# Block products for six inner tiles of the first feed-forward block, its state-space preparation in the last 44 products, and a re-ordered mixer

## The chip, the core and the metric

The kernel runs on one core of a Trainium2 chip. The metric is the device time of one execution in microseconds (us); three runs of the kernel before took 1043.52, 1045.11 and 1045.87 us, median 1045.11. The engines are called as in the profile: PE (TensorE matmul), PEld (its weight loads), DVE (VectorE), ACT (ScalarE), POOL (GpSimd), SP (the queue that issues the loads).

## What is computed

One block on x (512 frames x 1024 channels, float32) with a conditioning vector c: three sub-layers, each a normalised and modulated h with a gated residual.

```
mod = silu(c) @ w_ada + b_ada                       # 9 vectors of 1024
h = modulate(rms_norm(x, g1), mod[0], mod[1]);  x += 0.5*mod[2]*swiglu(h, w1_in, w1_out)
h = modulate(rms_norm(x, g2), mod[3], mod[4])
u_pool, u_ssm, gl_pool, gl_ssm = split(h @ w_in)
y = sigmoid(gl_pool)*(multiscale_pool(u_pool) @ w_pool_up) + sigmoid(gl_ssm)*(s5_mixer(u_ssm) @ w_ssm_up)
x += mod[5] * (y @ w_out)
h = modulate(rms_norm(x, g3), mod[6], mod[7]);  x += 0.5*mod[8]*swiglu(h, w3_in, w3_out)
return rms_norm(x, g_final)
```

swiglu(h) = (silu(a) * b) @ w_out with a, b = h @ w_in, 2816 inner channels: 22 *inner tiles* of 128, each with an a and a b product. The S5 part is a complex diagonal state space, 32 groups of 64 states; its discretised coefficients and their powers up to 127 frames are computed from the parameters in the kernel ("state-space preparation").

## The kernel before

**Layout.** Activations lie transposed: channels on the 128 partitions, 512 frames along the free axis, so h is 8 tiles of 128x512. Weights come from memory in float32, each tile is split into a high part (ACT cast, `wh`, L1327, in `split_hi`) and a low part (DVE subtraction, `wl`, L1335, in `split_lo`), and so are the activations (HH/HL for h, GHA/GLA and GC for the gated inner tiles). `mm3` (L265 to L268) makes each product from three matmuls: high x high, high x low, low x high.

**Units.** All work is a list of `Unit`s, each with its weights, its matmuls and what follows. The main loop (L1371 on) emits, for unit i: `pre`, the split of the weights of unit i+2 and loads beyond it (`prefetch`), the matmuls, `post`, perhaps a step of the adaLN dots (`ada_step`: one load of 512 KB and one 128x1024 dot on DVE, L132, with a small update of gates or scales), and in the first block one entry of the list `fill`. Every engine works through its instructions in the order in which they are emitted. A *plain* unit has 1024 weight columns, 24 matmuls of 512 columns; an *out* unit of n inner tiles has 3n.

**First block** (`ffn(0, ...)`, units 0 to 76). `group6` (L281) takes seven column tiles at once while h is still being made (`make_h1`, L222); then come plain units in `BLOCKS` of 6, 5, 5 and 6 inner tiles, each followed by out units that add to the residual X (L660); the last two, in `tail` (L340), are split into halves of 256 columns, interleaved with the next norm (column sums L202, row broadcast L216). `keep_warm(WARM[i])` (L1365 to L1368) puts dummy matmuls between the steps of the first norm.

**State-space preparation.** `fill` starts behind unit 18: the parameter loads (`ssm_load`), then 181 small DVE operations, 10 a unit (`SMALL`, recorded in `small`, all shown at L721) from unit 20 on. POOL builds tables of powers by doubling (`ssm_table(k)`, L912 to L917, k = 0 to 6, each six operations, the largest 128x1024), which use scratch that also holds results of the small operations. Then four batches: `ssm_batch_pool(b)` (L930 to L944) on POOL, and four units later `ssm_batch_pe(b)` on PE (transposes L951, products L956) with `ssm_batch_m(b)` (copies and diagonals, L969 to L971). A batch has six units: POOL's part is in the first and PE's in the last of them.

**Mixer** (`mixer()`, order written by hand at L1217 on). u units make the pool input, pf units the state-space input, gp and gs the gates; `si` (`ssm_in`, L1015), `sc` (`ssm_scan`, L1031: scans L1037) and `so` are the state-space steps on PE, DVE and POOL; `pw` multiplies the pooled tiles by pool_w (`pw_unit`, L1160 and the splits that follow), and `up` multiplies the result by w_pool_up.

**Third sub-layer** (`ffn_seven`, L458). Here 18 inner tiles are made in nine pairs by seven block products instead of eight (Winograd's form, 2x2 blocks): h is also needed as sums and differences of its blocks (`h_sums`, POOL, L248 to L251; split later), and weight blocks likewise (POOL, L517 to L519). `product` (L495 to L499) makes three 256-column matmuls; a pair has 56 products, in four halves of two units each (`half_units`: `split1`, `split2`), with sums behind them in `post1`, `done_a` and `done_b`. The second operands of a half lie in four slots.

Of the kernel before, what the change touches and what calls it, by code (L numbers as in the profile page):

```python
# [16 lines left out]
P = 128  # L17
# [3 lines left out]
BLOCKS = ((0, 6), (6, 11), (11, 16), (16, 22))  # L21
# [5 lines left out]
SMALL = 10  # L27
WARM = (6, 7, 1, 3)
# [17 lines left out]
class Unit:  # L46
    def __init__(self, src, cols, mm, pre=None, post=None):
# [3 lines left out]
        self.kind = 0  # L51
# [3 lines left out]
def block_kernel(ctx, tc, a, out):  # L55
# [96 lines left out]
    ada_jobs = []  # L152
# [10 lines left out]
    ada_loaded, ada_done = [0], [0]  # L163

    def ada_step():
# [6 lines left out]
        while ada_loaded[0] < len(ada_jobs) and ada_loaded[0] - ada_done[0] < 2:  # L172
            ada_load(ada_jobs[ada_loaded[0]][0])
            ada_loaded[0] += 1
# [47 lines left out]
    def make_h1(s, k, part):  # L222
# [6 lines left out]
        S.activation(out=HH[:, k, cs], in_=t[:, cs], func=AF.Identity, bias=shift_col(s, k))  # L229
        if s == 2:  # L230
# [10 lines left out]
    def h_sums(kp):  # L241
        if not sums:
            sums["h"] = big("SH", [P, 4, 4, T // 2], F32R, "PM")
            sums["l"] = big("SL", [P, 4, 4, T // 2], F32R, "QM")
        t = TB.rearrange("p r q c -> p (r q c)")[:, 1024 * kp:1024 * kp + 1024].rearrange("p (s t) -> p s t", s=4)
        f0, f1 = HF[2 * kp % 4], HF[(2 * kp + 1) % 4]
# [5 lines left out]
        late_splits.append(lambda: put_split(sums["h"][:, kp], sums["l"][:, kp], t))  # L252

    def make_h2(s, k, t, part):
# [5 lines left out]
        if s == 2 and k % 2 and made[k] == T and made[k - 1] == T and k // 2 not in made.setdefault("sums", []):  # L260
            made["sums"].append(k // 2)
            h_sums(k // 2)
# [195 lines left out]
    def ffn_seven(s, w6, win, wout, wend):  # L458
# [1054 lines left out]
```

## Time and profile before

| | |
|---|---|
| median of three runs | 1045.11 us (1043.52 to 1045.87) |
| profiled execution | 1044.0 us, of which the span 1042.2 |
| PE, DVE, ACT, POOL busy | 1026.7, 727.5, 392.0, 348.7 us |
| matmul groups with 512 and 256 columns, L266 to L268 | largest two: 536 and 308 per line |
| seven-product matmuls, L499 | three operand forms of 216 are the largest |
| weight splits wl, L1335 | 164, 195.3 us |
| adaLN dots, L132 | 50, 72.9 us |

In a row of the profile, `out<-in` are the tiles written and read (buffer numbers left out), then shape, count, and, in brackets, how long the engine had been idle and what released it. Spans of a window are followed by busy times of the five engines, the granted PE clock (1.00 is full), the share of the DMA engines and GB/s.

### The profile page before, as it was taken

The numbers are of one execution on the slowest core, as the hardware profiler recorded it, in microseconds if no ns is written. First come the engines' busy times: TensorE is split into PE (matmuls) and PEld (weight loads), VectorE is DVE, ScalarE is ACT, GpSimd is POOL, SyncE is SP. The second block draws the span as 40 slices with busy tenths as digits, with TensorE's granted clock in tenths as the row PEclk, the third lists the DMA queues.
The fourth block names the chain that finished last, engine by engine and source line by source line (L and its number), as shares of the span: only waits on it lengthen the run. The fifth ranks groups of instructions, "written<-read, shape, count | busy, mean of one in ns | idle before, by whom it ended". The sixth has DMA issues, their size and how long they took to land.

```text
span 1042.2 us, 14304 instructions
## 1 busy us (share of the span) xinstructions
PE 1026.7 (99%) x5514; PEld 872.5 (84%) x5514; DVE 727.5 (70%) x1127; ACT 392.0 (38%) x595; POOL 348.7 (33%) x309
## 2 busy tenths in 40 slices
PE   9999999999999999998999999999999999999996
PEld 7788888788888889886888887887899989988986
DVE  6956678989665655669924588365899948975843
ACT  4252222222232243584143333255545424432443
POOL 0000200499652411045600000133587705832312
PEclk9999999999999999999999999999999999999999
DMA  9664544445426432412336455222332522431222
GB/s 348 222 207 157 185 162 136 147 143 187 149 101 218 152 107 66 131 52 81 101 102 205 147 193 182 61 74 79 128 125 86 189 61 76 151 109 45 83 76 81
DMA packets 46310, 138.23 MB, mean 133 GB/s; under 512 B 5281, under 2 KB 9505, under 8 KB 46242
## 3 DMA queue, kind: packets, MB, share of 16 engines
q1 hardware_dynamic: 46242, 137.32, 38.9%
q8 instruction: 43, 0.70, 0.3%
q14 instruction: 25, 0.20, 0.1%
HBM read 134.15 MB, written 3.15 MB: 132 GB/s over the span
## 4 chain that ended last, share of the span: by engine, by line
PE 89%; DVE 5%; ACT 3%; issue 1%; DMA 0%; SPq 0%; DVEq 0%; ACTq 0%
PE ps L266 21%; PE ps L268 21%; PE ps L267 20%; PE ps L499 17%; PE ps L295 7%; DVE wl L1335 1%; ACT U L1010 1%; DVE ev L719 1%; ACT wh L1327 1%; PE ps L956 1%; DVE ev L225 1%; PE ps L1055 1%; ACT HH L229 1%; PE ps L202 1%; DVE PM L1037 1%
## 5 line engine op out<-in xcount | busy, mean ns | idle before, releaser
L1335 DVE TENSOR_TENSOR wl<-raw,wh 128x1024 fp32r<-128x1024 f32 (+4 forms) x164 | 195.3, 1194 | 83.9 <-ACT wh L1327 83.3
L1327 ACT CAST wh<-raw 128x1024 fp32r<-128x1024 f32 (+4 forms) x166 | 150.8, 913 | 162.2 <-PE ps L267 111.3
L268 PE MATMUL ps<-HH,wl 128*128 128x512 f32 (+1 forms) x536 | 208.1, 388 | 2.3 <-DVE wl L1335 2.3
L266 PE MATMUL ps<-HH,wh 128*128 128x512 f32 (+1 forms) x536 | 208.9, 390 | 0.0
L267 PE MATMUL ps<-HL,wh 128*128 128x512 f32 (+1 forms) x536 | 208.2, 388 | 0.0
L268 PEld LDWEIGHTS ps<-HH,wl 128*128 128x128 f32 x536 | 100.5, 187 | 25.8 <-DVE wl L1335 2.8
L267 PEld LDWEIGHTS ps<-HL,wh 128*128 128x128 f32 x536 | 100.5, 188 | 23.3 <-DVE HL L719 0.7
L266 PEld LDWEIGHTS ps<-HH,wh 128*128 128x128 f32 x536 | 100.5, 188 | 23.1 <-issue 0.4
L268 PE MATMUL ps<-GHA,wl 128*128 128x512 f32 (+1 forms) x308 | 118.3, 384 | 1.3 <-DVE wl L1335 1.3
L266 PE MATMUL ps<-GHA,wh 128*128 128x512 f32 (+1 forms) x308 | 118.7, 385 | 0.0
L267 PE MATMUL ps<-GLA,wh 128*128 128x512 f32 (+1 forms) x308 | 117.9, 383 | 0.0
L660 DVE SCALAR_TENSOR_TENSOR X<-ps,MOD,X 128x512 f32<-128x512 f32 (+1 forms) x78 | 55.1, 706 | 64.8 <-PE ps L268 64.7
L186 POOL TENSOR_TENSOR ACC<-ACC,ev 128x512 f32<-128x512 f32 x15 | 19.7, 1311 | 222.3 <-ACT ev L185 222.3
L132 DVE CUSTOM_DVE_ANT_0 ADA<-ADA,C,COL 128x1024 f32<-128x1024 f32 x50 | 72.9, 1458 | 0.0
L268 PEld LDWEIGHTS ps<-GHA,wl 128*128 128x128 f32 x308 | 57.8, 188 | 14.9 <-DVE wl L1335 2.4
L267 PEld LDWEIGHTS ps<-GLA,wh 128*128 128x128 f32 x308 | 57.8, 188 | 12.7 <-DVE GLA L272 0.3
L266 PEld LDWEIGHTS ps<-GHA,wh 128*128 128x128 f32 x308 | 57.8, 188 | 12.5 <-issue 0.4
L499 PE MATMUL ps<-SH,wl 128*128 128x256 f32 x216 | 60.5, 280 | 0.0
L499 PE MATMUL ps<-SH,wh 128*128 128x256 f32 x216 | 60.3, 279 | 0.0
L499 PE MATMUL ps<-SL,wh 128*128 128x256 f32 x216 | 60.2, 279 | 0.0
L517 POOL TENSOR_TENSOR MISC<-MISC 128x512 f32<-128x512 f32 x18 | 31.7, 1760 | 80.2 <-DMA MISC<-w_f_in 80.2
L271 ACT CAST GHA<-ev 128x512 fp32r<-128x512 f32 x24 | 14.9, 621 | 80.0 <-DVE ev L412 72.7
(253 smaller groups left out, 2136.4 us busy)
## 6 DMA issues: line engine op xcount, KB each, us to landing
ADA<-w_ada SPq DMA_DIRECT2D x50, 512.0 KB, 3.5
raw<-w_f_in SPq DMA_DIRECT2D x39, 512.0 KB, 4.3
raw<-w_f_out SPq DMA_DIRECT2D x38, 384.0 KB, 3.7
raw<-w_in SPq DMA_DIRECT2D x18, 512.0 KB, 3.8
MISC<-w_f_in SPq DMA_DIRECT2D x18, 512.0 KB, 3.5
raw<-w_f_out SPq DMA_DIRECT2D x16, 320.0 KB, 3.9
MM<-w_f_in SPq DMA_DIRECT2D x9, 512.0 KB, 3.6
ADA<-w_f_in SPq DMA_DIRECT2D x9, 512.0 KB, 3.5
```

Of the source, the lines that this page charges most:

```text
L132: V.tensor_tensor_reduce(out=t, in0=t, in1=C, scale=1.0, scalar=bada[:, n:n + 1], op0=ALU.mult, op1=ALU.add, accum_out=MOD[:, n:n + 1],)
L186: eng.tensor_tensor(out=acc[:, cs], in0=acc[:, cs], in1=sq[:, cs], op=ALU.add)
L266: E.matmul(pst, wh, xh, start=first, stop=False)
L267: E.matmul(pst, wh, xl, start=False, stop=False)
L268: E.matmul(pst, wl, xh, start=False, stop=last)
L271: S.copy(out=hi, in_=src)
L295: E.matmul(pst[m][:, cs], w_[:, w], x_, start=first and n == 0, stop=n == 2 and k == KT - 1)
L499: E.matmul(out_, w_[:, i, w], x_, start=first and n == 0, stop=last and n == 2, skip_group_check=True)
L517: G.tensor_tensor(out=c[:, 1:3], in0=c[:, 4:7:2], in1=c[:, 3:5], op=ALU.subtract)
L660: V.scalar_tensor_tensor(out=X[:, d, cs], in0=p[:, cs], scalar=MOD[:, s * 24 + 16 + d:s * 24 + 17 + d], in1=X[:, d, cs], op0=ALU.mult, op1 ...
L1327: S.copy(out=hi[:, 0:u.cols], in_=t)
L1335: eng.tensor_tensor(out=lo[:, 0:u.cols], in0=t, in1=hi[:, 0:u.cols].bitcast(F32), op=ALU.subtract)
```

## The change

It does five things.

- *First block.* `ffn` goes; `ffn_seven` serves both blocks. In the first one `group6` is as before, then plain units for tiles 3 to 5, out(0 to 5); six tiles in three pairs by seven block products (units 21 to 44) with three slots for the second operands instead of four; out(6 to 11) (45 to 52); plain units for 12 to 17 (53 to 64), out (65 to 72), plain for 18 to 21 (73 to 80), out (81 to 86) and a tail with four inner tiles. The block has 89 units instead of 77. h's sums are also made for it: `make_h1` has an additional ACT operation of 128x512 per tile, and the 16 POOL operations of `h_sums` stand after `group6`.
- *State-space preparation.* `fill` starts behind unit 45 (`n_fill`): 14 entries of 13 small operations (`NSMALL`, `SMALL`; units 46 to 59), the tables behind units 60 to 63, the batches' POOL parts behind units 65, 70, 75 and 80 and their PE parts behind 69, 74, 79 and 84. A batch has five units instead of six. The buffers PM, QM, TB and ACC are allocated anew there.
- *adaLN dots.* The eight gate dots of the first block join the list; one step is behind each of the units 8 to 18, and one behind every unit from 53 to 80 (before: behind 1024-column units from 16 on).
- *Mixer order.* The units stay the same, the list is written as below.
- *Start.* `WARM` is (6, 9, 2, 4) instead of (6, 7, 1, 3).

```diff
-BLOCKS = ((0, 6), (6, 11), (11, 16), (16, 22))
-SMALL = 10
-WARM = (6, 7, 1, 3)
+SMALL, NSMALL = 13, 14
+WARM = (6, 9, 2, 4)
...
+        if s == 0:
+            S.activation(out=MISC[:, T * k:T * k + T], in_=t, func=AF.Identity, bias=shift_col(s, k))
...
+            if s == 0:
+                third.append(pst[6])
+                for kp in range(4):
+                    h_sums(0, kp)
...
+        if s == 0:
+            units.append(plain(win[0], 1, 3, third))
+            for f in (4, 5):
+                hold = []
+                units.extend([plain(win[2 * f - 7 + ab], ab, f, hold) for ab in range(2)])
+            for u in units[-4:]:
+                u.pre = lambda: late_splits.pop(0)()
+            out_units(0, 6)
+            seq = []
+            for n in range(3):
+                seq.extend(pair(n, slot_of(6 + 2 * n), 5))
...
+            marks.append(len(units))
+            out_units(6, 12)
+            for f in range(12, 22):
+                if f == 18:
+                    out_units(12, 18)
+                hold = []
+                units.extend([plain(win[17 + 2 * (f - 12) + ab], ab, slot_of(f), hold) for ab in range(2)])
+            out_units(18, 22, range(6), True)
+            tail(s, wout[6, :, 18 * P:], wout[7, :, 18 * P:], 4, lambda k: gslots[k])
...
-    fill = [ssm_load, None]
-    fill += [some(SMALL)] * -(-len(small) // SMALL)
-    fill += [tables(0, 1, 2, 3), tables(4), tables(5), None, tables(6), None, None]
+    fill = [ssm_load]
+    fill += [some(SMALL)] * NSMALL
+    fill += [tables(0, 1, 2, 3), tables(4), tables(5), tables(6), None]
     for b in range(4):
-        fill += [lambda b=b: ssm_batch_pool(b)] + [None] * 4 + [lambda b=b: (ssm_batch_pe(b), ssm_batch_m(b))]
+        fill += [lambda b=b: ssm_batch_pool(b), None, None, None, lambda b=b: (ssm_batch_pe(b), ssm_batch_m(b))]
...
-        units.extend([u_unit(0), pf[3], u_unit(1), pf[2], si[0], gp[0], sc[0], gp[1], pf[0], pf[1], si[1], gp[2], sc[1], gp[3], pw_unit()])
-        units.extend([si[2], gp[4], sc[2], up[0], gp[5], si[3], up[1], sc[3], gp[6], up[2], so[0], gp[7], up[3]])
+        units.extend([u_unit(0), pf[3], u_unit(1), pf[2], gp[0], si[0], gp[1], sc[0], gp[2], pf[0], pf[1], gp[3], si[1], gp[4], sc[1]])
+        units.extend([pw_unit(), gp[5], si[2], up[0], sc[2], gp[6], up[1], si[3], gp[7], sc[3], up[2], so[0], up[3]])
...
-        if i >= 16 and (u.cols == 1024 if i < n_ffn1 else i >= n_gate):
+        if i == n_fill + KT:
+            ada_limit[0] = len(ada_jobs)
+        if 8 <= i <= 18 or n_fill + KT <= i < n_ffn1 - KT or i >= n_gate:
             ada_step()
```

The changed kernel's line numbers differ: the small operations are L742 (before L721) and L740 (L719), the weight subtraction L1368 (L1335), the dot L131 (L132), the residual L682 (L660), the tables L944 to L949, the batches' copy L1003 (L971), the scan L1067 (L1037), the pool product's post L1190 (L1160).

*The last of the small operations on DVE.* First before, behind the product of unit 37 (PM is the small operations' buffer, X the residual):

```order
L1335 TENSOR_TENSOR wl<-raw,wh 128x1024
L660 SCALAR_TENSOR_TENSOR X<-ps,MOD,X 128x512
L721 TENSOR_TENSOR PM<-PM 128x16 x2
L721 TENSOR_TENSOR PM<-PM,MISC 128x16
L721 TENSOR_TENSOR PM<-PM 128x16 x2
L721 TENSOR_TENSOR PM<-PM,MISC 128x256 x2
```

And now, behind unit 59 (ADA is the dot's operand, MOD its result):

```order
L1368 TENSOR_TENSOR wl<-raw,wh 128x1024
L131 ISA ADA,MOD<-ADA,C,COL 128x1024
L131 ISA MOD 128x1
L742 TENSOR_TENSOR PMs<-PMs 128x16 x3
L742 TENSOR_TENSOR PMs<-PMs,MISC 128x16
L742 TENSOR_TENSOR PMs<-PMs 128x16 x2
```

The residual update in front of the last small operations gives way to an adaLN dot; the second of the two (before) and the third of the three (now) is the 172nd small operation.

*DVE ahead of the first batch's copy*, before (units 49 to 51) and now (units 67 to 69):

```order
L1335 TENSOR_TENSOR wl<-raw,wh 128x640
L660 SCALAR_TENSOR_TENSOR X<-ps,MOD,X 128x512
L1335 TENSOR_TENSOR wl<-raw,wh 128x640
L660 SCALAR_TENSOR_TENSOR X<-ps,MOD,X 128x512
L971 COPY MM<-ps 32x512
```

```order
L682 SCALAR_TENSOR_TENSOR X<-ps,MOD,X 128x512
L131 ISA ADA,MOD<-ADA,C,COL 128x1024
L131 ISA MOD 128x1
L1368 TENSOR_TENSOR wl<-raw,wh 128x768
L682 SCALAR_TENSOR_TENSOR X<-ps,MOD,X 128x512
L131 ISA ADA,MOD<-ADA,C,COL 128x1024
L131 ISA MOD 128x1
L1003 COPY MM<-ps 32x512
```

A dot stands behind every out unit there now. Between the 172nd operation and that copy there were 14 weight subtractions (nine of 1024 columns, five of 640) and 10 dots; now there are 10 subtractions (three of 1024, seven of 768) and 10 dots.

*DVE in the mixer*, around the pool product's weights (128x512), the second scan and the post of the pool product; before:

```order
L719 TENSOR_TENSOR ev<-TB,ps 128x512 x4
L1335 TENSOR_TENSOR wl<-raw,wh 128x512
L1037 SCALAR_TENSOR_TENSOR PM<-RHO,PM 128x128 x8
L719 TENSOR_TENSOR ev<-TB,PM 128x512 x4
L1335 TENSOR_TENSOR wl<-raw,wh 128x1024 x2
L1160 TENSOR_SCALAR ev<-ps,COL 128x512 x4
```

and now:

```order
L1368 TENSOR_TENSOR wl<-raw,wh 128x512
L740 TENSOR_TENSOR ev<-TBs,ps 128x512 x4
L1368 TENSOR_TENSOR wl<-raw,wh 128x1024
L1067 SCALAR_TENSOR_TENSOR PMs<-RHO,PMs 128x128 x8
L740 TENSOR_TENSOR ev<-TBs,PMs 128x512 x4
L1368 TENSOR_TENSOR wl<-raw,wh 128x1024
L1190 TENSOR_SCALAR ev<-ps,COL 128x512 x4
L740 TENSOR_TENSOR GLA<-ev,GHA 128x512 x4
```

The pool product's subtraction moved ahead of the second state-space step's operations, and the two of the following products moved to either side of the scan.

More of the change, by code (lines that the diff above doesn't have):

```diff
@@ L150, in half_gate @@
         )
-    ada_jobs = []
+    ada_jobs = [(16 + d, lambda d=d: half_gate(0, d, d + 1)) for d in range(8)]
     for k in range(8):
@@ L573, in half_units, with pair @@
             u1 = Unit(src, 1024, mm1, None, post1 if kh else None)
-            u1.load, u1.split, u1.kind = load, split1, 1
+            u1.load, u1.split, u1.kind, u1.np2 = load, split1, 1, np2
             u2 = Unit(src, 768, mm2, None, pr.done if kh else None)
-            u2.split, u2.twin, u2.kind = split2, u1, 2
+            u2.split, u2.twin, u2.kind, u2.np2 = split2, u1, 2, np2
             return u1, u2
-        def pair(n, slot):
+        def pair(n, slot, w0):
             pa, pb = Pair(), Pair()
@@ L613, in slot_of @@
         def slot_of(f):
+            if s == 0:
+                return f % 6
             return f if f < 4 else (f - 4) % 6 - 2 if (f - 4) % 6 > 1 else 4 + (f - 4) % 6
@@ L635, in out_units @@
             units.extend([out_unit([d], f0, f1, wout[d, :, f0 * P:f1 * P], [], lastb=lastb) for d in ds])
+        if s == 0:
+            units.append(plain(win[0], 1, 3, third))
[8 more added lines that the diff above has]
+                seq.extend(pair(n, slot_of(6 + 2 * n), 5))
+            for i in range(6):
+                units.extend(seq[i][0])
+                if i:
+                    units.extend(seq[i - 1][1])
+            units.extend(seq[5][1])
+            marks.append(len(units))
[7 more added lines that the diff above has]
+            tail(s, wout[6, :, 18 * P:], wout[7, :, 18 * P:], 4, lambda k: gslots[k])
+            return
         hold = []
-        units.extend([plain(3, ab, 3, hold) for ab in range(2)])
+        units.extend([plain(win[ab], ab, 3, hold) for ab in range(2)])
         n = len(units)
@@ L810, in block_kernel @@
     stage = {}
+    small = []
     def ssm_load():
+        nonlocal PM, QM, TB, ACC
+        PM = big("PMs", [P, 2, NPAIR, P], F32, "PM")
+        QM = big("QMs", [P, NPAIR, 2, P], F32, "QM")
+        TB = big("TBs", [P, 2, NPAIR, P], F32, "TB")
+        ACC = big("ACCs", [P, T], F32, "ACC")
+        vq.kept = small
+        for f in (ssm_small1, ssm_small2, ssm_small3, ssm_small4, ssm_small5):
+            f()
+        vq.kept = None
         nc.sync.dma_start(out=prm, in_=a["ssm"])
@@ L1421, in block_kernel @@
         if i == n_ffn1 - 1:
-            assert not fill, len(fill)
+            assert not fill and not small, (len(fill), len(small))
     rb = ev()
```

159 lines of the change are left out of this document (73 added, 86 removed).

## Prediction

> **What bounds the kernel now.** I read the page first: busy times, slices, the chain that ended last.
>
> ```profile
> span 1042.2 us, 14304 instructions
> PE 1026.7 (99%) x5514; PEld 872.5 (84%) x5514; DVE 727.5 (70%) x1127; ACT 392.0 (38%) x595; POOL 348.7 (33%) x309
> DVE  6956678989665655669924588365899948975843
> POOL 0000200499652411045600000133587705832312
> PE 89%; DVE 5%; ACT 3%; issue 1%; DMA 0%; SPq 0%; DVEq 0%; ACTq 0%
> ```
>
> TensorE (PE) is busy for 1026.7 of 1042.2 us, and the 15.5 us that are left lie mostly ahead of its first product and behind its last one. So only two things change the time: the matmuls that PE issues, and any moment at which it finds an operand missing. No other engine is near its limit on average; POOL is at 0.9 in slices 8 to 10 (182 to 261 us), which is where the state-space tables are made beside the first block, and that will matter. Next I read windows, to price PE's two kinds of product (columns: window, length, busy time and instructions of PE, weight loads, DVE, ACT, POOL, then clock, DMA share, GB/s).
>
> ```profile
> 126.60:177.00 50.40, 50.40 (x217) 40.49 (x216) 37.26 (x116) 13.38 (x18) 0.00 (x0) 1.00 0.45 159
> 766.60:786.40 19.80, 19.80 (x170) 19.80 (x170) 19.10 (x23) 9.41 (x13) 18.49 (x15) 1.00 0.27 89
> 766.00:826.00 60.00, 60.00 (x510) 60.00 (x510) 58.39 (x72) 28.39 (x38) 48.64 (x37) 1.00 0.36 124
> ```
>
> Plain products of 512 columns in the first block: 50.40 us for 216 steps, 0.233 us each. One pair of inner tiles in the third sub-layer, by seven block products: 168 matmuls of 256 columns, 19.8 us (170 records in 19.80 us, 0.117 us each). In that stage PE never idles, but DVE is busy for 58.39 of 60 us, so there is little room left.
>
> **The change, part by part.** *Products.* Six inner tiles of the first block were 12 plain units of 24 matmuls: 12 x 24 x 0.233 = 67.1 us. They become three pairs, 3 x 19.8 = 59.4 us. All other products stay. **-7.7 us**, all of it on PE's path.
>
> *State-space preparation.* The 181 small DVE operations, the POOL tables and the four batches now run beside the last 44 products of the first block. What counts is when POOL may run through the long tables and when PE arrives at the first batch.
>
> ```profile
> 203.25 0.38 DVE L721 TENSOR_TENSOR PM<-PM 128x16 f32<-128x16 f32 x2
> 203.71 0.41 POOL L913 TENSOR_TENSOR PM<-TB,MISC 128x128 f32<-128x128 f32 x1 [5.43 <-DVE PM L721]
> 261.07 1.69 POOL L944 TENSOR_SCALAR MISC<-MISC 64x64 f32<-64x64 f32 x4
> 203.70:262.80 59.10, 59.10 (x255) 47.50 (x254) 51.74 (x49) 14.92 (x21) 56.83 (x43) 1.00 0.47 164
> 271.45 0.39 PE L268 MATMUL ps<-GC,wl 128*128 128x512 f32 x1
> 271.69 1.03 PE L951 MATMUL ps<-IDN,MISC 128*128 128x128 f32 x8
> 272.65 1.94 PE L956 MATMUL ps<-QM,MISC 128*32 128x128 f32 x16
> 201.49 0.39 PE L268 MATMUL ps<-GC,wl 128*128 128x512 f32 x1
> ```
>
> The table with 128 columns a pair shares its scratch with the small operations, so POOL sits idle for 5.43 us at L913 until the 172nd of them (the second at 203.25) ends. From there POOL works without a gap (56.83 of 59.10 us busy) until the last operation of the first batch ends at 261.07 + 1.69 = 262.76: a chain of 59.1 us. PE comes to the batch's transposes at 271.69 and to its products at 272.65, so the batch is 9.9 us early. The operation that releases POOL ends 1.8 us after the last matmul of its unit (201.49 + 0.39), and from there to the transposes PE has 14 units, 69.8 us.
>
> Now the 172nd operation stands behind unit 59, and the batch's products behind unit 69. Between lie five plain units (24 matmuls) and five out units of six tiles (18 matmuls): 210 x 0.233 = 48.9 us, 21 us less cover than before. Does POOL's chain get shorter too? Its length comes from what DVE does beside it:
>
> ```profile
> 238.15 3.25 POOL L917 TENSOR_TENSOR TB<-PM 128x1024 f32<-128x1024 f32 x1
> 239.09 3.40 DVE L1335 TENSOR_TENSOR wl<-raw,wh 128x1024 fp32r<-128x1024 f32 x1
> 201.46 1.22 DVE L1335 TENSOR_TENSOR wl<-raw,wh 128x1024 fp32r<-128x1024 f32 x1
> 198.97 0.81 DVE L1335 TENSOR_TENSOR wl<-raw,wh 128x640 fp32r<-128x640 f32 x1
> 241.36 1.61 POOL L930 TENSOR_TENSOR MISC<-MISC 128x256 f32<-128x256 f32 x1
> 252.17 0.62 POOL L930 TENSOR_TENSOR MISC<-MISC 128x256 f32<-128x256 f32 x1
> L132 DVE CUSTOM_DVE_ANT_0 ADA<-ADA,C,COL 128x1024 f32<-128x1024 f32 x50 | 72.9, 1458 | 0.0
> ```
>
> The same weight subtraction takes 1.22 us where POOL is idle and 3.40 us beside a 128x1024 table; the same POOL operation takes 0.62 or 1.61 us. One waits for the other, so POOL's chain is its own work plus most of the two-operand DVE work that falls into it. In before that is nine subtractions of 1024, two of 640 and nine adaLN dots: 9 x 1.22 + 2 x 0.81 + 9 x 1.46 = 25.7 us, and four small ones. Now, counted in the new order, it is three of 1024, seven of 768 (0.95 us, between 0.81 and 1.22), and ten dots: 3.7 + 6.7 + 14.6 = 25.0 us, and three small ones. With 0.7 us for a small one this is 1.5 us less: a chain of 57.6 us. The release lags its unit by 2.5 us (1.8, and 0.7 more since a dot of 1.46 stands ahead of the small operations in place of a residual update of 0.74). So the batch is done 2.5 + 57.6 = 60.1 us after unit 59, while PE gets to its products after 48.9 + 1.0 (transposes, which need only the batch's first half). **PE waits 10.2 us.** Bounds: 4 if a quarter of the two-operand work (6 of 25 us) slips past POOL, 13 if the release lags by 3.3 and the chain is as long as before. The Trainium skill, "SBUF — State Buffer", section "Who interferes with whom", calls the port pair that DVE and GpSimd share an exclusive lock, held for the whole instruction, and says that a DVE instruction with two SBUF inputs contends with GpSimd reads. The rows 3.40 against 1.22 and 1.61 against 0.62 agree; it speaks against this change, which puts a dot behind every unit of this stage.
>
> A wait of this length also reaches the clock.
>
> ```profile
> 1034.15 0.71 PE L216 MATMUL ps<-IDN,rc 128*128 128x128 f32 x4 [0.55 <-DVE rc L210]
> 1036.00:1042.00 6.00, 0.00 (x0) 0.00 (x0) 1.19 (x2) 0.00 (x0) 0.61 (x1) 0.59 0.54 181
> ```
>
> After the last matmul (ends 1034.86) the mean granted clock of the next window is 0.59: full until about 1037.1 and half from there ((0.59 - 0.5) / 0.5 x 6 = 1.1 us). So 2.2 us of idle bring the clock down, and 10 us do. No row shows a restart in mid-kernel; if the return takes as long as the fall it costs 1.1 us, if twice as long as that again some 3; I take **2.0 us** (0 to 4). The Trainium skill, "TensorE: Matmul & The Clock Gate", section "What's actually happening", has about 3.4 us of sustained activity before the full rate is back; by that the loss would be 1.7 us, and the sum 0.3 lower.
>
> The later batches: one took POOL 21.4 us beside this load (241.36 to 262.76), and five units, 21 to 28 us, now lie between two batches, where six lay before. The delay of the first moves PE back by the 12 us just counted, and POOL goes straight on. I put them at nothing; without that cover the last two would wait 1 to 3 us each.
>
> *Mixer order.* Two waits stand in the mixer now:
>
> ```profile
> 477.64 0.79 DVE L1335 TENSOR_TENSOR wl<-raw,wh 128x512 fp32r<-128x512 f32 x1
> 478.48 0.50 PE L268 MATMUL ps<-GHA,wl 128*128 128x512 f32 x1 [1.34 <-DVE wl L1335]
> 478.35 3.71 DVE L1037 TENSOR_TENSOR_SCAN PM<-RHO,PM 128x128 f32<-128x128 f32 x8
> 484.38 2.35 DVE L1335 TENSOR_TENSOR wl<-raw,wh 128x1024 fp32r<-128x1024 f32 x2
> 485.65 0.50 PE L268 MATMUL ps<-HH,wl 128*128 128x512 f32 x1 [2.32 <-DVE wl L1335]
> 490.09 2.49 DVE L719 TENSOR_TENSOR GLA<-ev,GHA 128x512 fp32r<-128x512 f32 x4
> ```
>
> The pool product's and the next gate product's weights are subtracted late, behind four 128x512 operations and a scan of 3.71 us. In the new order those subtractions stand ahead of them: 1.34 + 2.32 and the half-filled starts around them, 4.0 us, go. What is late next is the first product that reads the pool branch's low halves (L719 at 490.09): in the new order it follows after one gate and one state unit, and DVE has another subtraction of 1.2 us and a scan ahead of it. I take a new wait of 2.3 us, the size of the second one: **-1.7 us** (-4 to +1).
>
> *Start.*
>
> ```profile
> 11.39 1.87 PE L202 MATMUL ps<-ONE,ACC 128*128 128x1 f32 x8 [0.40 <-DVE ACC L186]
> 17.40 1.49 PE L1368 MATMUL ps<-ONE 128*128 128x128 f32 x6
> 19.21 2.22 PE L295 MATMUL ps<-HH,wh 128*128 128x512 f32 x7 [0.32 <-ACT HH L229]
> ```
>
> Two more dummies ahead of L202 (0.25 us each by the row at 17.40) take the place of its 0.40 us wait, and one more each at two later places that of 0.32 us: **+0.5 us** (-2 to +1).
>
> *Tail* of the first block.
>
> ```profile
> 402.88 0.28 PE L268 MATMUL ps<-GC,wl 128*128 128x256 f32 x1
> 403.22 1.30 PE L295 MATMUL ps<-HH,wh 128*128 128x256 f32 x6
> ```
>
> Four tiles instead of six: two products fewer between the norm's steps. The wait there is 0.34 - 0.12 = 0.2 us now, and six 256-wide matmuls of 0.12 us go in front of it. **+0.5 us** (0 to 1.5).
>
> *At nothing*, by these rows:
>
> ```profile
> 19.00:25.00 6.00, 5.70 (x21) 4.04 (x21) 5.96 (x10) 1.62 (x3) 0.00 (x0) 1.00 1.03 411
> L271 ACT CAST GHA<-ev 128x512 fp32r<-128x512 f32 x24 | 14.9, 621 | 80.0 <-DVE ev L412 72.7
> L250 POOL TENSOR_TENSOR TB<-ADA x2: 1455/1584/1714, 695.8 to 714.9; 128x256 f32<-128x256 f32 x2
> ```
>
> One more ACT copy of h per tile in the first group (0.6 us; ACT is used for 1.62 of 6 us there); 16 POOL sums of 128x256 (1.6 us each at most, 25 us together; POOL is empty there, and the last is needed at unit 12, after three more products of 5.6 us than the first at unit 9); their splits, which ACT and DVE make in those units. The SP queue carries the same weight bytes, with the state-space parameters 27 units later, behind loads issued two or three units ahead; it moves 160 GB/s in the plain stage and has moved 411. If the sums came one operation late, PE would wait 1.6 us.
>
> Sum: -7.7 + 10.2 + 2.0 - 1.7 + 0.5 + 0.5 = **+3.8 us**. The profiled run took 1044.0 us (span 1042.2 and 1.8 around it), the median is 1045.1; from the median, **1049 us**. About 0.2% (2.1 us) is what a measurement of this kernel can tell from no change.
>
> **The rivals.** *The preparation stays hidden* (faster). If POOL's chain needs less than 47 us, no wait comes, and -7.7 - 1.7 + 1.0 gives 1036.7. For it speaks that 59.1 less all of the two-operand work beside it (25.7 + 4 x 0.7 = 28.5 us) would leave POOL 31 us of its own; against it that nothing in the new order takes dots or subtractions out of that stage. *The wait is shorter*: 6 to 10 us with what it costs the clock, so that gain and wait cancel: 1045.1 - 8.4 + 8 = 1045. For it speaks that in out units DVE has more gaps for POOL than in plain ones. *Further waits* (slower still): the first block's pair stage has only three slots for second operands and DVE at 58 of 60 us; a slip of 2 us a pair beyond the first would add 4 to 6 us: 1054. It decides if a second operand's split ends later than the twin product's start. The change could also give less than it says if PE paced the 256-wide products slower than 0.117 us; the window shows that it doesn't.
>
> **How the numbers follow.** Forecast (wait of about 10 us and a clock fall) 0.47, at 1046 to 1053; shorter wait 0.22, at 1042 to 1047; hidden 0.20, at 1036 to 1038; further waits 0.11, at 1053 to 1058. The hidden case and half of the last can't both be left out, which would be over 2 in 10, so the range goes from 1036 to 1055; the likeliest case's own is 1046 to 1053. Faster by over 0.2% (below 1043.0): 0.20 + 0.07 = 0.27. Slower by over 0.2% (above 1047.2): 0.11 and most of the forecast, 0.38 of 0.47, together 0.49. The same: 0.24.
>
> **What would show it.** In the changed profile: three pairs of seven-product matmuls (504 of 256 columns) at 0.117 us and no PE wait in it; a PE wait of 8 to 12 us at the first batch's products (L988), put down to POOL, with a clock below 1 in its slice; POOL busy without a gap for 55 to 60 us ahead of that; no waits at the pool and gate products of the mixer, one of 2 us at the first pool-up product. Wrong would be: no wait at L988 (then the lock between DVE and POOL is weaker here than I took it), or waits on PE in the three pairs.

## The result and the profile after

The changed kernel takes **1058.4 us** (median of four runs, 1055.6 to 1062.4), the kernel before 1044.9 us in the same sessions: a ratio of 1.0132 (95% interval 1.0109 to 1.0154), 13.5 us slower (11.4 to 16.1 by the interval). The forecast was 1049 us with a range up to 1055. It is slower, as was forecast, and by more than three times as much.

The page of the profiled execution (1056.55 us):

```profile
span 1054.8 us, 14911 instructions
PE 1025.6 (97%) x5726; PEld 879.8 (83%) x5726; DVE 770.1 (73%) x1183; ACT 406.8 (39%) x617; POOL 416.5 (39%) x361
DVE  7977877779996655659953579556799957965843
POOL 0341653204998752044420000233597715732312
PE 70%; DVE 13%; POOL 6%; ACT 5%; DMA 2%; issue 2%; SPq 0%; DVEq 0%; ACTq 0%; POOLq 0%
```

PE's busy time is almost what it was (1025.6 against 1026.7 us), although the products got shorter: matmuls that run at half clock are counted in it. What the span gained is time in which PE waits. The chain that ended last says who it waits for: PE had 89% of it and has 70%, DVE went from 5 to 13% and POOL from nothing to 6%. POOL is at 0.8 to 0.9 in slices 11 to 13 (264 to 343 us) and DVE at 0.9 in slices 10 to 12 (237 to 316 us), so that both are busy at the same time, as forecast; but DVE is at 0.7 or more in all of the first twelve slices.

The waits of PE (total, times, longest) name the engine that ended each:

```profile
PE ps L274 <- ACT GC L279: 3.9, 1, 3.9
PE ps L988 <- POOL MISC L976: 3.5, 2, 3.0
PE ps L275 <- DVE GLA L740: 2.1, 1, 2.1
PE ps L303 <- ACT wh L1360: 1.6, 3, 1.0
PE ps L201 <- DVE ACCs L740: 1.6, 1, 1.6
PE ps L480 <- ACT ev L581: 1.5, 1, 1.5
...
PE ps L480 <- DVE wl L280: 1.1, 2, 0.8
```

Before, the only waits of a microsecond or more past the start were the mixer's two of 1.3 and 2.3 us. Now there are five places: the first group (L303), the pairs (L480), the state-space preparation (L274 on GC, and L988), the tail (L201) and the mixer (L275 on GLA).

**The preparation.** POOL's chain, from the wait for the small operations to the end of the first batch:

```profile
260.93 0.41 POOL L945 TENSOR_TENSOR PMs<-TBs,MISC 128x128 f32<-128x128 f32 x1 [9.00 <-DVE PMs L742]
...
316.78 1.69 POOL L976 TENSOR_SCALAR MISC<-MISC 64x64 f32<-64x64 f32 x4
```

It takes 316.78 + 1.69 - 260.93 = 57.5 us, against 57.6 in the forecast. But it isn't what PE meets first. DVE's instructions in the same stretch, around unit 64:

```profile
280.48 2.92 DVE L131 CUSTOM_DVE_ANT_0 ADA<-ADA,C,COL 128x1024 f32<-128x1024 f32 x1
...
283.33 2.65 DVE L1368 TENSOR_TENSOR wl<-raw,wh 128x768 fp32r<-128x768 f32 x1
285.90 3.42 DVE L131 CUSTOM_DVE_ANT_0 ADA<-ADA,C,COL 128x1024 f32<-128x1024 f32 x1
...
291.82 0.67 DVE L420 TENSOR_TENSOR ev<-ev,ps 128x512 f32<-128x512 f32 x1
```

A dot that takes 1.28 us where POOL is idle (at 42.90 us) takes 2.9 to 3.4 us beside the 128x1024 tables, and a subtraction of 768 columns, about 1 us by the forecast's estimate, takes 2.6. DVE falls behind; the last operation shown, which multiplies the a and b halves of an inner tile, was due when unit 64 ended at 285.6 and comes 6 us late at 291.82, and the high half of that inner tile later still. PE, at unit 65, needs it:

```profile
288.93 0.40 PE L276 MATMUL ps<-GC,wl 128*128 128x512 f32 x1
293.19 0.80 PE L274 MATMUL ps<-GC,wh 128*128 128x512 f32 x1 [3.87 <-ACT GC L279]
294.25 0.80 PE L275 MATMUL ps<-GC,wh 128*128 128x512 f32 x1 [0.27 <-DVE GC L280]
294.85 0.63 PE L276 MATMUL ps<-GC,wl 128*128 128x512 f32 x1
295.27 0.63 PE L274 MATMUL ps<-GHA,wh 128*128 128x512 f32 x1
...
317.65 0.41 PE L988 MATMUL ps<-QMs,MISC 128*32 128x128 f32 x2 [3.02 <-POOL MISC L976]
318.52 2.60 PE L988 MATMUL ps<-QMs,MISC 128*32 128x128 f32 x14 [0.46 <-POOL MISC L976]
```

The wait of 3.9 us is followed by matmuls that start 0.43 us apart instead of 0.23: the clock has fallen, for the 5.5 us from 293.2 to 298.7. When PE comes to the batch's products at 314.6, 3.0 + 0.5 us are left to wait. The clock in the windows around the two waits:

```profile
288.00:300.00 12.00, 7.87 (x23) 5.59 (x22) 11.32 (x10) 2.18 (x3) 11.76 (x7) 0.72 0.39 127
313.00:325.00 12.00, 8.52 (x42) 6.47 (x41) 5.45 (x10) 2.63 (x5) 11.08 (x18) 0.86 0.43 140
```

**The pairs.** The window of the three pairs, units 21 to 44:

```profile
121.50:185.00 63.50, 60.72 (x506) 59.91 (x505) 49.76 (x75) 26.15 (x34) 31.31 (x31) 1.00 0.29 93
```

504 matmuls in 63.5 us, where 59.4 were forecast: PE's 60.7 us of work and 2.8 us of idle, most of it in the third pair:

```profile
171.81 0.39 PE L480 MATMUL ps<-HH,wl 128*128 128x256 f32 x1 [0.76 <-DVE wl L280]
180.46 0.36 PE L480 MATMUL ps<-HH,J 128*128 128x256 f32 x1 [1.50 <-ACT ev L581]
```

### The profile page after: what moved, and what is told of

The parts are those of the page before. It is cut to its first block, busy times and chain, and to the rows that moved or that the text cites. A ratio compares the mean times of both kernels' runs of the same rounds, so it can differ in the third digit from the quotient of the medians.

```text
span 1054.8 us, 14911 instructions
## 1 busy us (share of the span) xinstructions
PE 1025.6 (97%) x5726; PEld 879.8 (83%) x5726; DVE 770.1 (73%) x1183; ACT 406.8 (39%) x617; POOL 416.5 (39%) x361
## 4 chain that ended last, share of the span: by engine, by line
PE 70%; DVE 13%; POOL 6%; ACT 5%; DMA 2%; issue 2%; SPq 0%; DVEq 0%; ACTq 0%; POOLq 0%
PE ps L480 19%; PE ps L274 15%; PE ps L275 15%; PE ps L276 15%; PE ps L303 5%; DVE wl L1368 3%; ACT wh L1360 1%; DVE ev L740 1%; DVE ADA L131 1%; ACT U L1040 1%; DVE ev L224 1%; DVE HL L264 1%; DVE PMs L742 1%; DVE wl L280 1%; DMA QM<-w_ada 1%
## 5 line engine op out<-in xcount | busy, mean ns | idle before, releaser
L1368 DVE TENSOR_TENSOR wl<-raw,wh 128x1024 fp32r<-128x1024 f32 (+3 forms) x152 | 180.8, 1194 | 75.1 <-ACT wh L1360 75.1
L1360 ACT CAST wh<-raw 128x1024 fp32r<-128x1024 f32 (+3 forms) x154 | 138.2, 902 | 135.9 <-PE ps L275 99.3
L274 PE MATMUL ps<-HH,wh 128*128 128x512 f32 (+1 forms) x440 | 170.9, 388 | 0.0
L275 PE MATMUL ps<-HL,wh 128*128 128x512 f32 (+1 forms) x440 | 170.3, 387 | 0.0
L276 PE MATMUL ps<-HH,wl 128*128 128x512 f32 (+1 forms) x440 | 170.2, 387 | 0.0
L275 PE MATMUL ps<-GLA,wh 128*128 128x512 f32 (+1 forms) x308 | 119.2, 387 | 2.4 <-DVE GLA L740 2.1
L274 PE MATMUL ps<-GHA,wh 128*128 128x512 f32 (+1 forms) x308 | 120.0, 390 | 0.5 <-ACT GHA L1194 0.5
L275 PEld LDWEIGHTS ps<-HL,wh 128*128 128x128 f32 x440 | 82.5, 188 | 19.0 <-DVE HL L740 0.7
L274 PEld LDWEIGHTS ps<-HH,wh 128*128 128x128 f32 x440 | 82.5, 188 | 18.8 <-ACT PMs L984 0.2
L682 DVE SCALAR_TENSOR_TENSOR X<-ps,MOD,X 128x512 f32<-128x512 f32 (+1 forms) x78 | 55.0, 706 | 57.3 <-PE ps L276 57.0
L185 POOL TENSOR_TENSOR ACCs<-ACCs,ev 128x512 f32<-128x512 f32 x15 | 20.2, 1345 | 188.6 <-ACT ev L184 188.6
L131 DVE CUSTOM_DVE_ANT_0 ADA<-ADA,C,COL 128x1024 f32<-128x1024 f32 x58 | 86.2, 1486 | 0.0
L480 PE MATMUL ps<-SH,wl 128*128 128x256 f32 x288 | 80.6, 280 | 0.0
L480 PE MATMUL ps<-SH,wh 128*128 128x256 f32 x288 | 80.4, 279 | 0.0
L480 PE MATMUL ps<-SL,wh 128*128 128x256 f32 x288 | 80.3, 279 | 0.0
L275 PEld LDWEIGHTS ps<-GLA,wh 128*128 128x128 f32 x308 | 58.5, 190 | 16.0 <-DVE GLA L740 2.4
L274 PEld LDWEIGHTS ps<-GHA,wh 128*128 128x128 f32 x308 | 58.6, 190 | 13.5 <-ACT GHA L1194 0.6
L480 PE MATMUL ps<-HH,J 128*128 128x256 f32 x268 | 63.7, 283 | 1.5 <-ACT ev L581 1.5
```

Of the source, the lines that this page charges most:

```text
L131: V.tensor_tensor_reduce(out=t, in0=t, in1=C, scale=1.0, scalar=bada[:, n:n + 1], op0=ALU.mult, op1=ALU.add, accum_out=MOD[:, n:n + 1],)
L185: eng.tensor_tensor(out=acc[:, cs], in0=acc[:, cs], in1=sq[:, cs], op=ALU.add)
L274: E.matmul(pst, wh, xh, start=first, stop=False)
L275: E.matmul(pst, wh, xl, start=False, stop=False)
L276: E.matmul(pst, wl, xh, start=False, stop=last)
L480: E.matmul(out_, w_[:, i, w], x_, start=first and n == 0, stop=last and n == 2, skip_group_check=True)
```

## The experiments

The tests of the preparation come first, then the pairs, the start, the mixer and the first group, the tail, and at last all mends together.

**e1, the dots taken out of the tables' way.**

```diff
-        if 8 <= i <= 18 or n_fill + KT <= i < n_ffn1 - KT or i >= n_gate:
+        if 8 <= i <= 18 or n_fill + KT <= i < 60 or 70 <= i < n_ffn1 - KT or i >= n_gate:
+            ada_step()
+        if n_gate <= i < n_gate + 12:
             ada_step()
```

> The changed kernel with the ten adaLN dots behind units 60 to 69 taken away from there and done at the end of the mixer (two behind a unit). Theory A (DVE's two-operand work and POOL's chain hold each other up): without 10 dots of 1.5 us POOL's chain from the release to the end of the first batch falls from 57.5 to 43-48 us, the wait of PE for GC at unit 65 (3.9 us) and that at the first batch's products (3.5 us) both go, no fall of the clock there; 1046 to 1049 us. Theory B (POOL's chain has a length of its own, only its late release matters): the chain stays at 55 us or more, PE waits 8 us or more at the batch's products; 1055 us or more. The waits in the three pairs, the tail and the mixer stay under both.

Measured 1057.5 us, ratio 1.0118 (1.0104 to 1.0132): no gain in the time, and yet theory A's signs are there. POOL's chain and PE at the first batch's products:

```profile
261.27 0.41 POOL L945 TENSOR_TENSOR PMs<-TBs,MISC 128x128 f32<-128x128 f32 x1 [9.00 <-DVE PMs L742]
308.06 1.69 POOL L976 TENSOR_SCALAR MISC<-MISC 64x64 f32<-64x64 f32 x4
```

```profile
308.94 0.41 PE L988 MATMUL ps<-QMs,MISC 128*32 128x128 f32 x2 [1.01 <-POOL MISC L976]
309.81 1.72 PE L988 MATMUL ps<-QMs,MISC 128*32 128x128 f32 x14 [0.46 <-POOL MISC L976]
```

The chain is 48.5 us instead of 57.5 (43 to 48 were expected), there is no wait for GC, 1.5 us are left at the products, and the clock holds. But the dots went to units where DVE had no room either, the products of the mixer's second half:

```profile
630.62 0.50 PE L276 MATMUL ps<-OB,wl 128*128 128x512 f32 x1 [0.92 <-DVE wl L1368]
637.00 0.50 PE L276 MATMUL ps<-HH,wl 128*128 128x512 f32 x1 [0.51 <-DVE wl L1368]
640.25 0.50 PE L275 MATMUL ps<-HL,wh 128*128 128x512 f32 x1 [0.42 <-DVE HL L740]
645.34 0.80 PE L274 MATMUL ps<-HH,wh 128*128 128x512 f32 x1 [3.58 <-ACT HH L1225]
646.61 0.80 PE L275 MATMUL ps<-HL,wh 128*128 128x512 f32 x1 [0.48 <-DVE HL L740]
```

5.9 us of waits there and another fall of the clock give the gain back: by the trace, the stretch from the end of the pairs to the end of the first batch's products is 9.9 us shorter than in the changed kernel, and the mixer from the first product that reads OB on is 9.2 us longer. That a dot costs 1.5 us of DVE wherever it stands was left out of the expectation.

**e2, tables that read nothing.** The 12 operations of the two largest tables become memsets of the same sizes; the tables' values are left out.

```diff
+        if k >= 5:
+            for i in range(2):
+                G.memset(t1, 0.5)
+                G.memset(t2, 0.5)
+                G.memset(TB[:, i, :, n:2 * n], 0.5)
+            return
```

> The changed kernel with the two largest tables (128x512 and 128x1024) filled by memsets of the same size that read nothing; the tables' values are left out, the dots stay. Theory A (the lock between POOL's reads and DVE's second operand makes DVE late): beside the memsets the weight subtraction and the dots take 1.0 to 1.3 us instead of 2.6 and 3.4, DVE is not late at unit 65, the 3.9 us wait for GC goes, and so does that at the first batch; 1046 to 1049 us. Theory C (DVE is late by its own load, a dot behind each unit, whatever POOL does): the wait for GC stays at 3 us or more, and only the wait at the batch's products goes; 1052 us or more.

Measured 1046.0 us, ratio 1.0010 (1.0001 to 1.0020): **12.3 us** less than the changed kernel. All dots stay where they were, and DVE is on time (beside POOL's memsets, 271.7 to 277.2):

```profile
271.67 1.27 DVE L131 CUSTOM_DVE_ANT_0 ADA<-ADA,C,COL 128x1024 f32<-128x1024 f32 x1
...
272.87 1.22 DVE L1374 TENSOR_TENSOR wl<-raw,wh 128x1024 fp32r<-128x1024 f32 x1
274.54 0.69 DVE L420 TENSOR_TENSOR ev<-ev,ps 128x512 f32<-128x512 f32 x1 [0.45 <-PE ps L276]
```

1.27 instead of 3.42 us for a dot, 1.22 for a subtraction of 1024, and DVE waits for PE where it was 6 us behind it. No wait for GC, none at the batch. So DVE's own load does not explain the wait (theory C falls); the tables' reads do. The Trainium skill, "SBUF — State Buffer", section "Who interferes with whom", says that a DVE instruction with two SBUF inputs contends with a GpSimd instruction that reads SBUF and not with one that only writes it; this pair of runs agrees, 3.42 us beside the one and 1.27 beside the other. The memsets are also shorter than the tables (0.96 us against 2.2 to 3.0), so that the wait at the batch would have gone in any case; the wait for GC is what the run decides.

**e5, an earlier release.** `SMALL, NSMALL = 17, 11` and three more empty entries ahead of the batches, which stay in their places.

> The changed kernel with 17 small operations behind a unit instead of 13, so that they end behind unit 56 and the tables follow three units earlier; the batches stay where they are, and so do the dots. Theory A: POOL's chain starts some 15 us earlier and is as long as before (57 us), so the wait at the first batch's products (3.5 us) goes; but the lock makes DVE late all the same, so a wait of 2 to 5 us for a gate half stays at unit 65 or comes up among units 57 to 65; 1051 to 1056 us. Rival (only the late release is at fault): both waits go; 1045 to 1048 us.

Measured 1054.1 us, ratio 1.0094 (1.0081 to 1.0107), 4.3 us less than the changed kernel. PE in that stage:

```profile
256.89 0.50 PE L276 MATMUL ps<-HH,wl 128*128 128x512 f32 x1 [1.40 <-DVE wl L1368]
280.38 0.50 PE L276 MATMUL ps<-HH,wl 128*128 128x512 f32 x1 [0.82 <-DVE wl L1368]
...
296.09 0.50 PE L274 MATMUL ps<-GC,wh 128*128 128x512 f32 x1 [1.04 <-ACT GC L279]
297.25 0.50 PE L275 MATMUL ps<-GC,wh 128*128 128x512 f32 x1 [0.66 <-DVE GC L280]
```

The release comes at 250.69 instead of 260.93, the wait at the products is gone, and 3.9 us of waits for DVE remain, spread over units 59 to 65. As theory A had it: an earlier start helps the batch, and DVE still pays for the tables.

**e3, a fourth slot.** GC is free until the third pair ends; a slot for second operands is put there (`np2 = 4`), and the planner counts four.

```diff
+                if s == 0 and job["n"] == 3:
+                    g = big("J1D", [P, 2048], F32R, "GC")
+                    st8["p2"].append((by256(g[:, 0:768]), by256(g[:, 768:1536])))
...
+                if s == 0 and slot >= 4:
+                    new_gslots()
```

> The changed kernel with a fourth slot for the second operands of the first block's pairs (in GC, which is free until the third pair ends), as in the third sub-layer. Theory D (three slots make each buffer free one half later, so the next load, POOL's pre-sums and the split come late): the waits in the pairs (0.3, 0.2, 0.8 and 1.5 us, 3.8 us with their slow starts) fall below 1 us together; 1054 to 1056 us. Rival E (POOL and DVE are at their limit in this stage): they stay within 1 us of 3.8; 1058 us.

Measured 1054.4 us, ratio 1.0087 (1.0073 to 1.0101): **4.0 us** less than the changed kernel. The window of the pairs:

```profile
121.50:185.00 63.50, 63.50 (x524) 62.69 (x523) 57.64 (x76) 27.53 (x37) 38.90 (x33) 1.00 0.34 113
```

PE doesn't idle in it any more: the 504 matmuls at 0.118 us, and the first 20 of the out units behind them, fill it. Theory D holds: the fourth slot alone takes the waits away. How three slots bring them about is read from the kernel and not from a run: the second split of a half waits for the products three halves back, its buffer comes free late, and the load, POOL's sums and the first split of the half that is to follow in that buffer are late in turn. DVE is no nearer to its limit than in the third sub-layer.

**e4, the dummies alone.** The kernel before with `WARM = (6, 9, 2, 4)`.

> The kernel before with only the dummy matmuls of the change (6, 9, 2, 4). Theory F (the dummies bring the clock to full before the first column sums, which take 0.13 us each in place of 0.23): the first product starts at 17.1 instead of 19.2 us, 1.5 to 2.2 us faster than before. Rival G (the dummies cost what they replace): within 0.5 us of before.

Measured 1044.66 us against 1044.65, ratio 0.9995 (0.9984 to 1.0005). Rival G: no effect. The early start in the changed kernel's profile (first product at 17.1 us) is not the dummies' doing: with them the first product came at 19.8 us here, at 19.6 us in e5 and at 20.3 us in e9, and at 16.8 to 17.3 us in the other kernels that have them. The first column sums tell which it is, in e4 and in the changed kernel:

```profile
11.81 1.86 PE L202 MATMUL ps<-ONE,ACC 128*128 128x1 f32 x8
```

```profile
11.71 1.17 PE L201 MATMUL ps<-ONE,ACC 128*128 128x1 f32 x8
```

Eight of them take 1.86 us where the start is late and 1.17 where it is early. The clock records of the traces have the full clock from 12.0 us on in the changed kernel, from 20.5 us in e4, 19.8 in e5 and 19.6 in e9. e5 and the changed kernel are the same up to unit 45, so it is the execution and not the kernel that decides, and two to three microseconds of the start are chance.

**e6, the mixer's old order** in the changed kernel.

> The changed kernel with the mixer's old order. By the two profiles the old order's waits (1.5 and 2.5 us, for weight subtractions) come back and the new one's (0.6 and 2.3 us, at the first pool-up product) go: 1.1 us slower than the changed kernel, 1058 to 1060 us. Rival: the new order's wait also lets the clock fall, so the old order is the same or up to 1 us faster.

Measured 1061.0 us, ratio 1.0161 (1.0146 to 1.0176), 2.6 us more than the changed kernel. The two old waits are back:

```profile
491.71 0.50 PE L276 MATMUL ps<-GHA,wl 128*128 128x512 f32 x1 [1.36 <-DVE wl L1368]
498.87 0.50 PE L276 MATMUL ps<-HH,wl 128*128 128x512 f32 x1 [2.31 <-DVE wl L1368]
```

against 0.46 + 2.08 us of the new order at its first pool-up product. By waits the new order is worth 1.1 us, by time 2.6, but the two intervals overlap, and the traces say where the rest comes from. From the start of the mixer to the first product that reads YB, which lies behind both places, the changed kernel takes 162.4 us and e6 165.0, and e6's execution has a fall of the clock there (3.4 us from 499.7) that the changed kernel's has not. With the new order such a fall stands in the traces of e1, e2, e3, e5 and e11, which take 163.6 to 163.9 us; the kernel before, with the old order and no fall, takes 163.4. Like compared with like, the new order is worth 1.1 us, and the rival's fall of the clock behind its wait does come in some executions.

**e7 and e11, the sums held back.** One copy on POOL, which reads a column of h's last tile, stands ahead of the 16 sums. In e7 it writes a new tile of 4 bytes, in e11 a place that the sums overwrite.

```diff
+                z = big("Z", [P, 1])
+                G.tensor_copy(out=z, in_=HL[:, KT - 1, 0:1].bitcast(F32))
                 for kp in range(4):
                     h_sums(0, kp)
```

> The changed kernel with the 16 POOL sums of h held back until h's last tile is made (a copy of one column on POOL that reads it). Theory H (the sums read beside the first group's two-operand DVE work, which is at its limit there, and make it late): the waits of 0.7 and 1.1 us at 51 and 54 us go, the first split of unit 7 is not late; 1.5 us faster than the changed kernel. Rival I (the additional ACT copies make the split late): the waits stay at 1.8 us together.

> The changed kernel with the sums of h held back, without the additional tile. Theory H: the waits of 0.7 and 1.1 us in the first group stay away and the pace is 0.233 us: 1055 to 1057 us, 2 to 3 us faster than the changed kernel. If holding back is worth nothing: 1058 us.

e7 took 1053.5 us (ratio 1.0078, 1.0062 to 1.0094), 4.9 us less than the changed kernel, and this was more than theory H allowed. The cause is the tile (below). e11 took 1056.1 us (ratio 1.0113, 1.0099 to 1.0126), **2.3 us** less, which the intervals alone don't tell from nothing. The traces do: from the first product to the first out unit the changed kernel takes 70.9 us, e11 68.9 and the kernel before 68.3. In the first group of the changed kernel:

```profile
52.17 1.90 PE L303 MATMUL ps<-HH,wl 128*128 128x512 f32 x7 [0.52 <-DVE wl L1368]
55.02 1.20 PE L303 MATMUL ps<-HH,wh 128*128 128x512 f32 x4 [0.96 <-ACT wh L1360]
```

and in e11, without either wait:

```profile
51.39 1.80 PE L303 MATMUL ps<-HH,wl 128*128 128x512 f32 x7
53.03 1.80 PE L303 MATMUL ps<-HH,wh 128*128 128x512 f32 x7
```

In the changed kernel the sums ran from 44.3 us, beside a DVE that is at its limit there (a dot of 1.75 us and a subtraction of 1.61 at 48.8 and 50.5, 1.28 and 1.08 in e11).

**e12, a tail of four tiles**, alone, in the kernel before: `BLOCKS = ((0, 6), (6, 12), (12, 18), (18, 22))`.

> The kernel before with blocks of 6, 6, 6 and 4 inner tiles instead of 6, 5, 5 and 6, so that the first block's tail has four tiles, as in the changed kernel; the products are the same in number. If the tail with four tiles costs what the changed kernel's profile shows (waits of 0.4, 0.9, 1.7 and 0.3 us where before has 0.2, 0.2 and 0.3): 2 to 3 us slower, 1046.5 to 1047.5 us. If it costs what was forecast: 0.5 us slower, 1044.5 to 1045.2 us.

Measured 1048.1 us against 1045.5, ratio 1.0037 (1.0024 to 1.0049): **2.5 to 5 us** slower. Two of the tail's waits are those of the changed kernel (0.76 and 1.57 us there), and the third stands at the step that the forecast priced:

```profile
398.79 0.38 PE L268 MATMUL ps<-GHA,wl 128*128 128x256 f32 x1 [0.96 <-DVE wl L1335]
403.10 0.61 PE L202 MATMUL ps<-ONE,ACC 128*128 128x1 f32 x4 [1.48 <-DVE ACC L719]
406.53 1.30 PE L295 MATMUL ps<-HH,wh 128*128 128x256 f32 x6 [0.41 <-ACT HH L229]
```

By the traces the tail of e12 is 0.7 us longer than that of the kernel before although it has 24 matmuls of 256 columns (2.8 us) fewer, so four tiles cost 3.5 us there.

**e8, e9, e10: all mends, and the place of the weight tiles.** The mends are the fourth slot, the sums held back, no dots behind units 60 to 69 (some of them two behind a unit at the mixer's last gate products), `SMALL, NSMALL = 16, 12` with batches two units earlier, and `gp[6]` ahead of `up[0]`. e8 holds the sums back by way of the 4-byte tile, e9 without it. e10 is the kernel before with nothing but such a tile (GC is named ahead of it so that it stays where it was):

```diff
     RHO = big("RHO", [P, NPAIR])
+    gc = big("GC", [P, 4, T], F32R, "GC")
+    Z = big("Z", [P, 1])
+    V.memset(Z, 0.0)
```

> All mends together: four slots; sums held back; no dots behind units 60 to 69 (they go to the end of the mixer, before its GLU products); 16 small operations behind a unit, so that tables and batches come two to three units earlier; one gate product more ahead of the first pool-up product. If the causes add up, the waits of the first block (12.5 in the preparation, 3.8 in the pairs, 1.8 in the first group) go but for some 2 us, and of the mixer's 3 us one is left: 1058.4 - 12.5 - 3.8 - 1.8 - 2 + 2 = 1040 us (1037 to 1044), faster than the kernel before. If the mends give their work back elsewhere: 1046 us or more.

> The kernel of all mends, with the copy that holds the sums back written into their own buffer instead of a new 4-byte tile, so that the weight tiles lie where they lie in the kernel before (32 bytes past a multiple of 64). Theory J (the place of the weight tiles sets the pace of the matmuls: 0.227 us a 512-wide one in the two runs with that tile, 0.234 in all others): the pace is 0.234 again and the time 3 to 6 us longer than with the tile, 1041 to 1044 us, with the same waits. Rival K (holding the sums back or the chip makes the pace): the pace stays at 0.227 and the time at 1038 us.

> The kernel before with one 4-byte tile more ahead of the weight tiles, which moves them by 32 bytes; nothing else. Theory J: 512-wide matmuls at 0.227 to 0.230 instead of 0.233 us (some 2700 of them, 7 us), the 256-wide ones of the block products at 0.120 instead of 0.118 (1500, 3 us the other way): 1039 to 1042 us. Rival K: 1044 to 1045 us and the old pace.

| | us | ratio to before |
|---|---|---|
| e8, mends and tile | 1038.1 | 0.9928 (0.9913 to 0.9943) |
| e9, mends | 1041.1 | 0.9961 (0.9949 to 0.9973) |
| e10, before and tile | 1032.7 | 0.9885 (0.9871 to 0.9898) |

e9 is 17.3 us faster than the changed kernel and 4.1 us (0.39%) faster than before: the mends add up, and what the seven products save shows. e10 is a surprise: 4 bytes more in each partition make the kernel before 12 us faster than it was, and faster than all others. In the built programs the tile moves everything that lies behind it by 32 bytes: raw, `wh`, `wl` and the result tiles `ev` start 32 bytes past a multiple of 64 in the kernel before and in e9, and at a multiple of 64 with the tile. The plain products of the first block in e10:

```profile
124.00:174.00 50.00, 50.00 (x222) 41.41 (x221) 37.84 (x115) 13.40 (x20) 0.00 (x0) 1.00 0.44 157
```

222 matmuls in 50.00 us, where the kernel before has 216 in the window from 126 to 176 us: from start to start 0.227 against 0.234 us (medians). In the third sub-layer's pairs it is the other way:

```profile
754.00:814.00 60.00, 60.00 (x499) 59.83 (x498) 58.42 (x72) 28.34 (x38) 49.69 (x38) 1.00 0.39 132
```

499 instead of 510 in 60 us, 0.120 against 0.118 us. Theory J's signs are all there, and Rival K is out: the median step of the 512-wide matmuls is 0.227 us in the three kernels with the tile (e7, e8, e10) and 0.234 in all eleven without it. The gain of e10 is larger than expected, since there are more of these matmuls and more of the difference goes through: over its whole trace, the step falls from 0.2340 to 0.2288 us for some 3100 matmuls of 512 columns (16 us) and rises from 0.118 to 0.120 for some 1900 of 256 (4 us), and 16 less 4 is the measured 12.

One comparison inside the traces tells which of the moved tiles it is. In the third sub-layer's pairs the first operands lie in `wh` and `wl`, which moved, and the second ones in J, which starts at a multiple of 64 in both kernels. In the kernel before, the products from `wh` and `wl` take 0.117 us a step (847 steps) and those from J 0.120 (468 steps); in e10 both take 0.120. So the step goes with the place of the tile that PE loads as weights. For the 512-wide matmuls no run separates the weight tiles from the result tiles.

In the changed kernel with its mends the same tile is worth only 3 us (e8 against e9). By the two traces the faster step is worth 9 us in e8 (0.2342 to 0.2294 us for 2800 matmuls, the other way for 2400), and 4.5 us more of waits (12.8 against 8.3 us) and two falls of the clock, 1.7 us lost in each, which e9 has not, take most of that back. That DVE falls behind where PE runs faster fits where the waits stand (e8 has 0.7, 0.8 and 1.3 us in the preparation and 2.4 us in the mixer; e9 0.8 and 1.9 us); no run tests it.

## Why the prediction was wrong

By its own steps:

- **Products, -7.7 us: right.** With four slots the pairs have no idle time, and PE's rows show the forecast pace; e9 is faster than before once the waits are mended.
- **The wait of the preparation, 10.2 + 2.0 us: right in its cause and size, wrong in its place.** 12.2 were forecast, taking the tables' reads away gave 12.3 (e2). The chain was 57.5 us (forecast 57.6), the release at 260.9 came 3.1 us behind unit 59's last matmul (2.5). But half of the waiting was met at unit 65, as DVE's lateness, and not at the batch. The working counted what DVE does to POOL and not what POOL does to DVE: its own rows (3.40 us against 1.22) showed both directions. "A PE wait of 8 to 12 us at the first batch's products, put down to POOL" is therefore not in the profile; two waits and two falls of the clock are. That the size came out all the same is not luck: PE can't pass the batch before POOL's chain ends, so what it lost on the way (3.9 + 0.3 us of waits at unit 65, and half of the 5.5 us at half clock behind them) came off the wait at the batch, of which 3.0 + 0.5 us were left. Together these are 10.4 us, and 10.2 were forecast.
- **The clock, 2.0 us: right in mechanism and about in size.** The fall behind the batch's wait lasts 3.4 us (from 319.2) at half clock, 1.7 us lost. The forecast had one fall; the changed kernel's trace has three, the first at unit 65 and the last in the tail (3.4 us from 414.8).
- **"At nothing", the failed step.** The third pair's waits were a rival at 0.11, priced at 4 to 6 us, on top of the forecast: they cost 4.0 us (e3; 63.3 against 59.3 us for the pairs by the traces), and the place is the one named (three slots). "Waits on PE in the three pairs" was among the forecast's own signs of being wrong. The POOL sums in the first group were covered for POOL and for PE, but not for DVE, which they hold up: 2.0 us by the traces of e11, 2.3 by its times. The row by which they were put at nothing shows DVE busy for 5.96 of 6.00 us. At 0.11 such a slip was held unlikely, on the strength of the third sub-layer's pairs, which have a slot more. And stages that lose cover at the same time add up: pairs, first group and tail together are some 9 us beside the forecast's wait, more than the 6 us that the range allowed above it.
- **Tail, +0.5 us: 2.5 to 5 us** (e12; 3.5 by its trace). Two tiles fewer were priced by the wait that one step has now. In the changed kernel the waits came up at other steps, and the longest, 1.57 us, is for the sums of squares, which DVE finishes last.
- **Mixer, -1.7 us: right** in sign; -1.1 by waits and by the traces, the new wait of 2.1 us at the forecast place (2.3).
- **Start, +0.5 us: none** (e4: -1.7 to +0.5).

One reading of the working was off, and nothing in its sum rests on it: in the kernel before, POOL is at 0.9 in slices 9 and 10 (208 to 261 us) and at 0.4 in slice 8.

The sum with what was measured: -7.7 + 12.3 + 4.0 + 2.0 + 3.5 - 1.1 = 13.0 us, against 13.5. The rest is within what the intervals leave open.

## What to carry to other kernels

Where POOL and DVE both work with operands in SBUF beside a busy PE, price each shared stretch twice: what POOL's chain loses to DVE, and what DVE's queue loses to POOL, since PE may first meet the second. When several stages lose cover at once, add their waits; rivals in different places can come together. Where work is put at nothing, look at every engine that it touches, not only at the one that does it. And before a kernel is rebuilt to save matmuls, look at where its weight tiles lie: here 32 bytes were worth more (12 us) than the whole change could have been (9.4 us, by the forecast's two gains).

## What the runs showed of the hardware

- The place of the weight tiles in SBUF changes the pace of the matmuls. Moving the raw, high and low weight tiles and the result tiles together by 32 bytes, to a multiple of 64, changed the median step of 512-wide float32 matmuls from 0.234 to 0.227 us and the mean step of the 256-wide ones in the pairs from 0.118 to 0.120 us (e10 against the kernel before). In the pairs the step goes with the tile that holds the weights: products from `wh` and `wl` go from 0.117 to 0.120 us, those from J, which did not move, take 0.120 us in both. For the 512-wide ones it was not tried which of the moved tiles does it.
- POOL operations that read SBUF stretch a two-operand DVE instruction (a dot) from 1.27 to as much as 3.42 us; POOL memsets of the same size do not (e2).
- After a PE wait of 3.9 us the matmuls ran at 0.43 us a step, instead of 0.23, for 5.5 us.
- A wait of about 2 us brings the clock down in some executions and not in others: behind the mixer's wait of 2.1 us the traces of e1, e2, e3, e5 and e11 have a fall of 3.4 us, that of the changed kernel has none.
- The moment at which the clock comes up at the start differs from execution to execution: 12.0 us in the changed kernel, 19.8 in e5, which starts with the same instructions. The first product comes 2 to 3 us later with it, whatever the dummies (e4, e5, e9).
